# A transformer layer with retention, pooling and a convolutional MLP: score matmuls by row halves, other places of weight splits, an output stage in another order, a tail that works in PSUM

## The chip, the cores and the metric

The kernel runs on one core of one Trainium2 chip. The metric is the device time of one execution in microseconds, from the chip's own clock; of several executions the median is taken. A core has five engines that run side by side, each with its own instruction stream in a fixed order: PE (TensorE, matrix products, written into eight banks of PSUM), DVE (VectorE), ACT (ScalarE), POOL (GpSimd), and SP (SyncE), which here only issues transfers between HBM and SBUF. An instruction waits by semaphores for what it reads and for the buffers that it overwrites, and everything behind it on its engine waits with it.

## What is computed

One layer over 512 latent tokens (x, 512 x 1024) with 256 context tokens, all in float32. Cut to what matters:

```python
u = _layer_norm(x) * (1.0 + sc1) + sh1                 # sh, sc, g: SiLU(c) @ w_ada + b_ada, six rows
k, v, q, g, p_in, gate_a, gate_b = split(u @ w_in)     # context tokens: k and v alone
# retention: 8 heads, key width 64, value width 128, chunks of 128 tokens, two directions
scores = einsum('bnihd,bnjhd->bnhij', qc, kc) * decay_in
y = scores @ vc + (q * q_dec) @ s_prev                 # both directions, per-head norm, times silu(g)
ret = y @ w_branch_ret
pool = pool_mixer(p_in) @ w_branch_pool
mix = (sigmoid(gate_a) * ret + sigmoid(gate_b) * pool) @ w_out
x = _layer_norm(ALPHA * x + g1 * mix) * ln1_g + ln1_b
u2 = _layer_norm(x) * (1.0 + sc2) + sh2
h = depthwise_conv3x3(u2 @ w_up) + conv_b              # 5632 channels on an 8 x 64 grid
a, b = split(h)
x = _layer_norm(ALPHA * x + g2 * ((gelu(a) * b) @ w_down)) * ln2_g + ln2_b
```

## The kernel before

Each float32 product is made of three matmuls (`mm3`, lines 92 to 95): both operands are split into a rounded part (`hi`, written by ACT) and the rest (`lo`, a subtraction on DVE or POOL, line 83), and hi*hi, hi*lo and lo*hi are summed in PSUM. Weights come from HBM into rotating `raw` buffers (six) or `row` buffers (three), are split into `hi` and `lo` (two buffers each) and used once. In the steps of `run_steps` the split of the next weight is written ahead of the product of the present one.

The stages in order of time are: the modulation and norm of x, the first projections, k and v, then eight steps `ga_step` and eight `gb_step` (one 512-wide product each, 24 matmuls) that carry the retention of one head per step: `ret_a(h)` makes the head's scores, states and decayed queries, `ret_b(h)` and `ret_c(h)` a step later the output, its norm and its transposes. In `ret_a` one head's scores are four matmuls with 64 rows (line 632), since a head's q and k lie in one half of the 128 partitions: even heads in rows 0 to 63, odd heads in rows 64 to 127 of tile `t`. From `k_post` to the end of the `br` steps only SP is in the written order; a scheduler has placed the instructions of the other engines when the program was built.

Then eight `br_step` (24 matmuls each) and eight `bp_step` (12 matmuls each) merge the branches. Among them `prep_out` (line 755) loads and splits the eight row tiles of `w_out` for the output projection into four buffers `wo[0]` to `wo[3]`; the tables `BR_W` and `BP_W` name the step at which each one is prepared. `wo[2]` and `wo[3]` take the buffers S6 and S0, which hold the split input of the `br` steps until the last of these has ended. In the `bp` steps PE and SP are in the written order, the rest is scheduled.

The output stage is written out by hand for all engines: for each block `tb` of 128 tokens two products of 24 matmuls (`out_mm`), whose halves stay in PSUM (`zps`); residual and statistics on DVE; `out_x1a` (mean and `ln_scale`, whose two small instructions on POOL, lines 125 and 126, give the reciprocal deviation; a multiplication by ln1_g on DVE), `out_x1b` (the scale and ln1_b, statistics of the next norm, and again `ln_scale`), `out_norm` (the normalised block into `xr`), `out_tr` (eight transposes on PE, then modulation on ACT, and the `lo` part by POOL or DVE). In the shadow of this, `early_prep` splits the first six weights of the up-projection, and `first_half` multiplies them with the first two blocks (24 matmuls of 256 columns).

After the up-projection, the convolution and most of the down-projection (18 of 22 row tiles for all blocks) the tail goes block by block: `unit` makes the last four row tiles' products for a half of 512 columns (12 matmuls), `gated_add` multiplies by g2 into an SBUF buffer and adds it to `x1`; `quarters`, `norm_a` and `norm_b` are the statistics, the mean and ln2_g, and the scale, ln2_b and store. The last block's second half is made in two quarters of 256 columns.

```python
def prep_out(i, k):
    ...
    raw = load(row() if i >= 2 else raw4(), a["w_out"][2 * i + k])
    act.copy(w[:, 0, k, :], raw)
    sub(dve if k and i < 3 else pool, w[:, 1, k, :], raw, w[:, 0, k, :].bitcast(F32))
```

Of the kernel before, what the change touches and what calls it, by code (L numbers as in the profile page):

```python
# [45 lines left out]
def layer_kernel(ctx: ExitStack, tc: tile.TileContext, a: dict):  # L46
# [707 lines left out]
    def prep_out(i, k):  # L754
# [113 lines left out]
    def out_norm(tb):  # L868
        src = x1[:, tb, :]
# [250 lines left out]
    for f in range(2, N_FRONT):  # L1120
# [14 lines left out]
    def gated_add(z, ps, cs, eng, add):  # L1135
        t = t2((P, cs.stop - cs.start))
        if eng is act:
            act.copy(t, ps)
            pool.tensor_tensor(t, t, g2[:, cs], ALU.mult)
        else:  # L1140
            dve.tensor_tensor(t, ps, g2[:, cs], ALU.mult)
        add.tensor_tensor(z[:, cs], z[:, cs], t, ALU.add)
# [2 lines left out]
    gated_add(x1[:, end, :], banks[end][1], HALVES[1], act, pool)
    st = [t2((P, 4, 6)) for _ in range(NTB)]
    scale = {}

    def unit(tb, cs):
# [122 lines left out]
```

## Time and profile before

| | us |
|---|---|
| three runs | 844.09, 845.35, 846.95 |
| median | 845.35 |
| the profiled execution | 847.08 |
| its span, first to last instruction | 845.3 |
| PE busy | 811.7 |
| DVE busy | 545.3 |
| POOL busy | 405.8 |
| ACT busy | 363.3 |

The mean granted clock of TensorE over the span is 0.985 of full speed. The span leaves 1.8 us of the profiled execution outside. A timeline row gives the start in us from the span's beginning, the duration, engine, line and operation, output and inputs by the program's names without their numbers, the count of merged instructions, and in brackets how long the engine had idled before it and what ended that. PE's matmuls overlap in the pipeline, so their pace is read from the starts, not from the durations. Float32 matmuls that are not split (scores, states, transposes of other data) appear as two records each.

### The profile page before, as it was taken

The numbers are of one execution on the slowest core, as the hardware profiler recorded it, in microseconds if no ns is written. First come the engines' busy times: TensorE is split into PE (matmuls) and PEld (weight loads), VectorE is DVE, ScalarE is ACT, GpSimd is POOL, SyncE is SP. The second block draws the span as 40 slices with busy tenths as digits, with TensorE's granted clock in tenths as the row PEclk, the third lists the DMA queues.
The fourth block names the chain that finished last, engine by engine and source line by source line (L and its number), as shares of the span: only waits on it lengthen the run. The fifth ranks groups of instructions, "written<-read, shape, count | busy, mean of one in ns | idle before, by whom it ended". The sixth has DMA issues, their size and how long they took to land.

```text
span 845.3 us, 10601 instructions
## 1 busy us (share of the span) xinstructions
PE 811.7 (96%) x3865; PEld 676.7 (80%) x3865; DVE 545.3 (65%) x1033; ACT 363.3 (43%) x578; POOL 405.8 (48%) x303
## 2 busy tenths in 40 slices
PE   6989999999999999998999899999999999999993
PEld 4768877888888888887887898888888888888883
DVE  7948789783267773444566659877788877522148
ACT  4644527121544342323233557666666665233100
POOL 3745350030633230204333859988888888222145
PEclk9999999999999999999999999999999999999997
DMA  9940369864210006352404512232232223342002
GB/s 347 406 173 13 136 230 324 305 224 139 74 51 26 2 1 224 125 174 83 176 26 171 188 42 75 100 100 100 100 100 94 88 93 100 121 137 93 0 1 99
DMA packets 34068, 106.94 MB, mean 127 GB/s; under 512 B 4560, under 2 KB 5344, under 8 KB 34016
## 3 DMA queue, kind: packets, MB, share of 16 engines
q1 hardware_dynamic: 34016, 106.27, 35.9%
q8 instruction: 30, 0.49, 0.2%
q14 instruction: 22, 0.18, 0.1%
HBM read 104.14 MB, written 2.11 MB: 126 GB/s over the span
## 4 chain that ended last, share of the span: by engine, by line
PE 82%; DVE 7%; POOL 4%; ACT 3%; issue 2%; DMA 1%; SPq 0%; POOLq 0%; DVEq 0%
PE ps L95 24%; PE ps L94 24%; PE ps L93 24%; PE ps L356 3%; POOL S L83 2%; PE ps L632 1%; PE ps L668 1%; PE ps L669 1%; PE ps L638 1%; ACT t L896 1%; PE ps L635 1%; DVE raw L205 1%; DVE lo L83 1%; DMA S<-in_x 1%; PE ps L298 1%
## 5 line engine op out<-in xcount | busy, mean ns | idle before, releaser
L95 PE MATMUL ps<-S,lo 128*128 128x512 f32 (+1 forms) x560 | 217.4, 390 | 5.6 <-POOL lo L83 4.6
L93 PE MATMUL ps<-S,hi 128*128 128x512 f32 (+1 forms) x560 | 218.6, 390 | 1.0 <-ACT hi L88 1.0
L94 PE MATMUL ps<-S,hi 128*128 128x512 f32 (+1 forms) x560 | 217.4, 388 | 0.0
L83 POOL TENSOR_TENSOR lo<-raw,hi 128x1024 fp32r<-128x1024 f32 (+2 forms) x65 | 141.1, 2172 | 158.5 <-ACT hi L88 155.6
L990 DVE SCALAR_TENSOR_TENSOR t<-ps,convw,t 128x441 f32<-128x441 f32 (+1 forms) x258 | 163.9, 692 | 46.3 <-POOL t L988 46.1
L88 ACT CAST hi<-raw 128x1024 fp32r<-128x1024 f32 (+2 forms) x100 | 100.0, 1001 | 181.5 <-PE ps L95 67.7
L95 PEld LDWEIGHTS ps<-S,lo 128*128 128x128 f32 x560 | 106.0, 189 | 28.6 <-POOL lo L83 5.4
L93 PEld LDWEIGHTS ps<-S,hi 128*128 128x128 f32 x560 | 106.1, 189 | 22.6 <-ACT hi L88 1.5
L94 PEld LDWEIGHTS ps<-S,hi 128*128 128x128 f32 x560 | 106.0, 189 | 21.1
L988 POOL TENSOR_TENSOR t<-t,t 128x448 f32<-128x448 f32 x88 | 101.9, 1158 | 36.6 <-ACT t L1071 33.1
L94 PE MATMUL ps<-S,S 128*128 128x512 f32 (+1 forms) x308 | 112.4, 365 | 0.0
L95 PE MATMUL ps<-S,S 128*128 128x512 f32 (+1 forms) x308 | 112.3, 365 | 0.0
L93 PE MATMUL ps<-S,S 128*128 128x512 f32 (+1 forms) x308 | 111.7, 366 | 0.0
L83 DVE TENSOR_TENSOR lo<-raw,hi 128x1024 fp32r<-128x1024 f32 x37 | 50.0, 1351 | 70.0 <-ACT hi L88 69.9
L94 PE MATMUL ps<-lo,S 128*128 128x512 f32 x208 | 81.8, 393 | 0.0
L95 PE MATMUL ps<-hi,S 128*128 128x512 f32 x208 | 81.5, 393 | 0.0
L93 PE MATMUL ps<-hi,S 128*128 128x512 f32 x208 | 77.4, 392 | 1.7 <-ACT S L546 1.0
L83 POOL TENSOR_TENSOR S<-raw,S 128x1024 fp32r<-128x1024 f32 x21 | 50.5, 2405 | 43.5 <-ACT S L759 28.1
L1068 ACT ACTIVATE t<-ps,convb,convw 128x512 f32<-128x512 f32 x43 | 33.6, 781 | 76.5 <-PE ps L95 76.5
L95 PEld LDWEIGHTS ps<-S,S 128*128 128x128 f32 x308 | 58.3, 189 | 9.3
L94 PEld LDWEIGHTS ps<-S,S 128*128 128x128 f32 x308 | 58.4, 190 | 9.2
L93 PEld LDWEIGHTS ps<-S,S 128*128 128x128 f32 x308 | 58.4, 190 | 9.1
(212 smaller groups left out, 1085.0 us busy)
## 6 DMA issues: line engine op xcount, KB each, us to landing
raw<-in_w_up SPq DMA_DIRECT2D x44, 512.0 KB, 3.4
raw<-in_wada SPq DMA_DIRECT2D x32, 512.0 KB, 5.2
raw<-in_w_down SPq DMA_DIRECT2D x22, 512.0 KB, 3.3
S<-in_wada SPq DMA_DIRECT2D x16, 512.0 KB, 9.1
raw<-in_w_v SPq DMA_DIRECT2D x16, 256.0 KB, 4.4
raw<-in_w_ga SPq DMA_DIRECT2D x8, 512.0 KB, 4.5
raw<-in_w_gb SPq DMA_DIRECT2D x8, 512.0 KB, 3.3
raw<-in_w_br SPq DMA_DIRECT2D x8, 512.0 KB, 4.5
```

The costliest lines, as they stand in the source:

```text
L83: eng.tensor_tensor(out, x, y, ALU.subtract)
L88: act.copy(hi, raw)
L93: pe.matmul(out, lhsT=sh, rhs=mh, start=first, stop=False)
L94: pe.matmul(out, lhsT=sh, rhs=ml, start=False, stop=False)
L95: pe.matmul(out, lhsT=sl, rhs=mh, start=False, stop=last)
L205: dve.scalar_tensor_tensor(out_junk, raw, 1.0, silu_c, ALU.mult, ALU.mult, accum_out=mod[:, j:j + 1])
L298: pe.transpose(ps[:, j * P:(j + 1) * P], xs[:, tb, k * P:(k + 1) * P], ident)
L356: pe.matmul(g0[f], lhsT=w[:, f * P:(f + 1) * P], rhs=m[:, kt, :], start=kt == 0 and i == 0, stop=kt == NKT - 1 and i == 2)
L632: pe.matmul(sc[:, ns], lhsT=kT[rows, t, ns], rhs=qT[rows, t, ns], start=True, stop=True)
L988: pool.tensor_tensor(o, o, i, ALU.add)
L990: dve.scalar_tensor_tensor(o, i, w, o, ALU.mult, ALU.add)
L1068: act.activation(acc, src, AF.Identity, bias=convb[:, i:i + 1], scale=convw[:, i, 4:5])
```

## The change

Five things are changed.

1. **Scores.** When an even head comes, both heads of tile `t` get a bank, and their eight score matmuls are issued in turns, rows 0 to 63 and rows 64 to 127. The odd head finds its scores in `score`.
2. **Weight splits.** `w_out`'s row tiles are prepared at `br` steps 0, 1, 3, 4 and `bp` steps 0, 2, 4, 6, where it was 2, 2, 5, 5 and 0, 0, 3, 3. The `lo` part of the second half of `wo[2]` moves from DVE to POOL.
3. **Output stage.** `out_x1a` of blocks 1, 2 and 3 stands ahead of the transposes or the `early_prep` that it stood behind. Block 3's x1 stays in PSUM; `out_norm(3)` reads it there, stands behind `out_tr(2)`, and ACT copies it into `x1` afterwards.
4. **Regions.** The up-projection's seventh weight is prepared inside the region of the output stage.
5. **Tail.** Products by g2, the sum with `x1`, and statistics per half work in PSUM on DVE; `+EPS` moves from POOL to DVE. Block 0 and block 2 are finished on ACT (scale and mean) and POOL (ln2_g, ln2_b), block 1 on DVE (mean, ln2_g), ACT and POOL, block 3 on DVE. DVE, ACT and POOL are in the written order there. Eight stores of half blocks take the place of two of whole and four of half blocks.

```diff
-BR_W, BP_W = (2, 2, 5, 5), (0, 0, 3, 3)
+BR_W, BP_W = (0, 1, 3, 4), (0, 2, 4, 6)
-ORDT = (E_SP,)
+ORDT = (E_SP, E_DVE, E_ACT, E_POOL)
...
-        sc = bank()
-        for n in range(NTB):
-            ns = slice(n * P, (n + 1) * P)
-            pe.matmul(sc[:, ns], lhsT=kT[rows, t, ns], rhs=qT[rows, t, ns], start=True, stop=True)
+        if r == 0:
+            for i in range(2):
+                score[h + i] = bank()
+            for n in range(NTB):
+                ns = slice(n * P, (n + 1) * P)
+                for i in range(2):
+                    half_rows = slice(i * DK, (i + 1) * DK)
+                    pe.matmul(score[h + i][:, ns], lhsT=kT[half_rows, t, ns], rhs=qT[half_rows, t, ns],
+                              start=True, stop=True)
+        sc = score.pop(h)
...
-        sub(dve if k and i < 3 else pool, w[:, 1, k, :], raw, w[:, 0, k, :].bitcast(F32))
+        sub(dve if k and i < 2 else pool, w[:, 1, k, :], raw, w[:, 0, k, :].bitcast(F32))
...
-            z = x1[:, tb, cs]
+            z = ps if tb == NTB - 1 else x1[:, tb, cs]
...
         if tb == NTB - 1:
-            for cs in HALF:
-                dve.tensor_scalar(xr[tb][:, cs], src[:, cs], mu, rs, ALU.subtract, ALU.mult)
+            for hf in range(2):
+                dve.tensor_scalar(xr[tb][:, HALF[hf]], zps[tb, hf], mu, rs, ALU.subtract, ALU.mult)
+            for hf in range(2):
+                act.copy(x1[:, tb, HALF[hf]], zps[tb, hf])
             return
...
     out_mm(1, 1)
+    out_x1a(1)
     out_tr(0)
     out_x(2)
-    out_x1(1)
+    out_x1b(1)
...
     early_prep(2, pool)
+    out_x1a(3)
     early_prep(3, pool)
-    out_x1a(3)
+    out_x1b(3)
     early_prep(4, pool)
-    out_x1b(3)
-    out_norm(3)
     early_prep(5, pool)
     first_half(0)
     first_half(1)
     out_tr(2)
+    out_norm(3)
...
+    part = banks[NTB - 1][1]
+    dve.tensor_tensor(part, part, g2[:, HALVES[1]], ALU.mult)
+    dve.tensor_tensor(x1[:, NTB - 1, HALVES[1]], part, x1[:, NTB - 1, HALVES[1]], ALU.add)
...
+    def residual(tb, ps, cs):
+        dve.tensor_tensor(ps, ps, g2[:, cs], ALU.mult)
+        dve.tensor_tensor(ps, ps, x1[:, tb, cs], ALU.add)
+
+    def piece(tb, cs, n, of):
...
+        residual(tb, ps, cs)
...
+        dve.bn_stats(st[tb][:, n, :], ps)
+        parts[tb].append((ps, cs))
+
+    def block_scale(tb):
+        mv = small([P, 2])
+        dve.bn_aggr(mv, st[tb])
+        rs = small([P, 1])
+        dve.tensor_scalar(rs, mv[:, 1:2], EPS, None, ALU.add)
+        pool.tensor_tensor(rs, rs, neg_half, ALU.pow)
...
+    def centred(tb):
+        for ps, cs in parts[tb]:
+            dve.scalar_tensor_tensor(ps, ps, mean[tb], lng[:, cs], ALU.subtract, ALU.mult)
+
+    def finish_pool(tb):
+        nmr = small([P, 1])
+        dve.tensor_scalar(nmr, mean[tb], scale[tb], -1.0, ALU.mult, ALU.mult)
+        for ps, cs in parts[tb]:
+            act.activation(x1[:, tb, cs], ps, AF.Identity, bias=nmr, scale=scale[tb])
+        for ps, cs in parts[tb]:
             z = x1[:, tb, cs]
...
+            pool.tensor_tensor(z, z, lng[:, cs], ALU.mult)
+            pool.tensor_tensor(z, z, lnb[:, cs], ALU.add)
+            store(tb, cs)
+            yield
...
     for tb in range(end):
...
+        piece(tb, HALVES[0], 0, 2)
+        if tb == 1:
+            weave(finish_pool(0))
+        elif tb:
+            finish_act(tb - 1)
+        piece(tb, HALVES[1], 1, 2)
+        block_scale(tb)
+        if tb == 1:
+            centred(tb)
+    piece(end, HALVES[0], 0, 3)
+    late = finish_pool(end - 1)
+    next(late)
+    piece(end, QUARTERS[2], 1, 3)
+    piece(end, QUARTERS[3], 2, 3)
+    block_scale(end)
+    centred(end)
+    for i, (ps, cs) in enumerate(parts[end]):
+        dve.scalar_tensor_tensor(x1[:, end, cs], ps, scale[end], lnb[:, cs], ALU.mult, ALU.add)
+        if i != 1:
+            store(end, HALVES[min(i, 1)])
+        weave(late)
```

What the change does to the order on the engines is shown at three places. On PE, heads 2 and 3 of the retention, before (first fence) and now (second; line 636 is the new place of line 632, 641 and 644 of 635 and 638; `S0` is the tile with q and k, `S4` and `S6` hold v of the context and of the tokens):

```order
L95 MATMUL ps_316_2038<-S2_8_78,lo_300_1939 128x512
L632 MATMUL ps_319_2072<-S0_80_529 128x128 x4
L635 MATMUL ps_320_2077<-S4_169_1031,kdc_318_2067 128x128 x2
L638 MATMUL ps_321_2080<-S6_84_542,t2_317_2064 128x128 x4
...
L95 MATMUL ps_335_2144<-S2_8_78,lo_315_2035 128x512
L632 MATMUL ps_338_2178<-S0_80_529 128x128 x4
L635 MATMUL ps_339_2183<-S4_169_1031,kdc_337_2173 128x128 x2
```

```order
L95 MATMUL ps_316_2038<-S2_8_78,lo_301_1944 128x512
L636 MATMUL ps_319_2072<-S0_80_529 128x128
L636 MATMUL ps_320_2073<-S0_80_529 128x128
L636 MATMUL ps_319_2072<-S0_80_529 128x128
L636 MATMUL ps_320_2073<-S0_80_529 128x128
...
L641 MATMUL ps_321_2082<-S4_169_1031,kdc_318_2067 128x128 x2
...
L95 MATMUL ps_336_2149<-S2_8_78,lo_315_2035 128x512
L641 MATMUL ps_339_2183<-S4_169_1031,kdc_338_2178 128x128 x2
```

The four matmuls of head 3 (`ps_320` now) have moved up between those of head 2; at head 3's own place none are left.

On POOL, around the end of the `br` steps, before and now (`lo` of 128x512 is the split of the next `bp` weight; `S0` and `S6` are `wo[3]` and `wo[2]`):

```order
L83 TENSOR_TENSOR lo_494_3240<-raw_492_3237,hi_493_3239 128x512
L83 TENSOR_TENSOR S0_513_3340<-row_514_3341,S0_513_3340 128x1024
L83 TENSOR_TENSOR S6_498_3262<-row_499_3263,S6_498_3262 128x1024
L83 TENSOR_TENSOR lo_503_3274<-raw_501_3271,hi_502_3273 128x512
L83 TENSOR_TENSOR lo_507_3297<-raw_505_3294,hi_506_3296 128x512
L83 TENSOR_TENSOR S0_513_3340<-row_515_3345,S0_513_3340 128x1024
```

```order
L83 TENSOR_TENSOR lo_494_3240<-raw_492_3237,hi_493_3239 128x512
L83 TENSOR_TENSOR S0_517_3363<-row_518_3364,S0_517_3363 128x1024
L83 TENSOR_TENSOR S6_498_3262<-row_499_3263,S6_498_3262 128x1024
L83 TENSOR_TENSOR S6_498_3262<-row_508_3313,S6_498_3262 128x1024
L83 TENSOR_TENSOR lo_502_3270<-raw_500_3267,hi_501_3269 128x512
L83 TENSOR_TENSOR lo_506_3293<-raw_504_3290,hi_505_3292 128x512
L83 TENSOR_TENSOR S0_517_3363<-row_527_3414,S0_517_3363 128x1024
```

Between the `lo` of `bp` step 1 (`lo_494`) and that of `bp` step 2 stood two splits of 1024 columns, and now stand three; the third was DVE's.

On POOL, in the output stage from the statistics of block 3 on, before and now (`S7` and `S3` are the early up-projection weights, `S8` the `lo` part of the transposed blocks):

```order
L83 TENSOR_TENSOR S7_586_3812<-raw_585_3810,S7_586_3812 128x1024
L83 TENSOR_TENSOR S7_586_3812<-raw_587_3815,S7_586_3812 128x1024
L125 TENSOR_SCALAR sm_589_3821<-sm_588_3819 128x1
L126 TENSOR_TENSOR sm_589_3821<-sm_589_3821,neg_half_66 128x1
L83 TENSOR_TENSOR S3_591_3828<-raw_590_3826,S3_591_3828 128x1024
L125 TENSOR_SCALAR sm_594_3838<-sm_593_3836 128x1
L126 TENSOR_TENSOR sm_594_3838<-sm_594_3838,neg_half_66 128x1
```

```order
L83 TENSOR_TENSOR S7_586_3812<-raw_585_3810,S7_586_3812 128x1024
L125 TENSOR_SCALAR sm_588_3817<-sm_587_3815 128x1
L126 TENSOR_TENSOR sm_588_3817<-sm_588_3817,neg_half_66 128x1
L83 TENSOR_TENSOR S7_586_3812<-raw_589_3822,S7_586_3812 128x1024
L125 TENSOR_SCALAR sm_592_3833<-sm_591_3831 128x1
L126 TENSOR_TENSOR sm_592_3833<-sm_592_3833,neg_half_66 128x1
L83 TENSOR_TENSOR S3_594_3838<-raw_593_3836,S3_594_3838 128x1024
```

Each pair of small instructions (lines 125 and 126) of block 3 has moved ahead of one split of 1024 columns.

## Rows read from the trace of the kernel before

**Rows 1.** Windows of the core: length, busy time (instructions) of each engine, clock, DMA.

```profile
200.00:300.00 100.00, 100.00 (x576) 85.28 (x575) 55.38 (x150) 38.96 (x86) 34.07 (x26) 1.00 0.13 43
...
750.00:800.00 50.00, 50.00 (x223) 41.38 (x222) 9.81 (x8) 15.47 (x15) 9.60 (x4) 1.00 0.22 70
...
832.00:846.00 14.00, 0.00 (x0) 0.00 (x0) 9.38 (x15) 1.34 (x2) 7.25 (x7) 0.58 0.29 110
```

**Rows 2.** Timeline of PE around the scores of one head.

```profile
233.24 0.39 PE L95 MATMUL ps<-S,lo 128*128 128x512 f32 x1
233.55 1.16 PE L632 MATMUL ps<-S 64*128 64x128 f32 x8
234.64 0.71 PE L635 MATMUL ps<-S,kdc 128*128 128x128 f32 x4
235.19 1.06 PE L638 MATMUL ps<-S,t 128*128 128x128 f32 x8
236.08 0.60 PE L613 MATMUL ps<-ident,S 128*128 128x128 f32 x4
```

**Rows 3.** Timeline of PE at the third `bp` step.

```profile
397.45 0.39 PE L94 MATMUL ps<-S,hi 128*128 128x512 f32 x1
400.71 0.80 PE L95 MATMUL ps<-S,lo 128*128 128x512 f32 x1 [2.87 <-POOL lo L83]
...
404.22 0.39 PE L94 MATMUL ps<-S,hi 128*128 128x512 f32 x1
```

**Rows 4.** Timeline of POOL at the same place.

```profile
392.46 1.30 POOL L83 TENSOR_TENSOR lo<-raw,hi 128x512 fp32r<-128x512 f32 x1 [4.15 <-ACT hi L88]
393.71 5.72 POOL L83 TENSOR_TENSOR S<-row,S 128x1024 fp32r<-128x1024 f32 x2
399.39 2.50 POOL L83 TENSOR_TENSOR lo<-raw,hi 128x512 fp32r<-128x512 f32 x2
401.86 2.37 POOL L83 TENSOR_TENSOR S<-row,S 128x1024 fp32r<-128x1024 f32 x1
```

**Rows 5.** Timeline of DVE at the same place.

```profile
395.32 1.89 DVE L83 TENSOR_TENSOR S<-row,S 128x1024 fp32r<-128x1024 f32 x1
```

**Rows 6.** Timeline of PE in the output stage, its two waits.

```profile
452.92 1.09 PE L888 MATMUL ps<-ident,xr 128*128 128x128 f32 x8 [0.90 <-ACT xr L877]
...
476.97 0.28 PE L95 MATMUL ps<-S,S 128*128 128x256 f32 x1
479.32 1.09 PE L888 MATMUL ps<-ident,xr 128*128 128x128 f32 x4 [2.07 <-issue]
...
481.45 0.56 PE L93 MATMUL ps<-S,S 128*128 128x256 f32 x1
```

**Rows 7.** Timeline of POOL in the output stage, two of its small instructions.

```profile
446.38 0.22 POOL L125 TENSOR_SCALAR sm<-sm 128x1 f32<-128x1 f32 x1
...
471.64 0.22 POOL L125 TENSOR_SCALAR sm<-sm 128x1 f32<-128x1 f32 x1
```

**Rows 8.** Timeline of DVE in the output stage.

```profile
423.93 0.70 DVE L844 TENSOR_TENSOR ps<-ps,row 128x512 f32<-128x512 f32 x1 [2.20 <-PE ps L95]
...
447.28 0.75 DVE L860 SCALAR_TENSOR_TENSOR S<-ps,sm,row 128x512 f32<-128x512 f32 x1 [3.16 <-POOL sm L126]
...
472.55 0.75 DVE L860 SCALAR_TENSOR_TENSOR S<-ps,sm,row 128x512 f32<-128x512 f32 x1 [2.22 <-POOL sm L126]
...
476.65 3.98 DVE L873 TENSOR_SCALAR xr<-S,sm,sm 128x512 f32<-128x512 f32 x2 [1.00 <-POOL sm L126]
```

**Rows 9.** Timeline of PE, its last matmul.

```profile
831.49 0.28 PE L95 MATMUL ps<-S,S 128*128 128x256 f32 x1
```

**Rows 10.** Timeline of DVE in the tail.

```profile
836.01 0.40 DVE L1141 TENSOR_TENSOR t<-ps,row 128x256 f32<-128x256 f32 x1
...
840.87 1.41 DVE L1174 SCALAR_TENSOR_TENSOR S<-S,sm,row 128x512 f32<-128x512 f32 x2 [0.77 <-POOL sm L126]
```

**Rows 11.** Timeline of SP's queue, the last two stores.

```profile
841.65 0.99 SPq L1175 DMA_DIRECT2D out_x<-S  x2
```

More of the change, by code (lines that the diff above doesn't have):

```diff
@@ L606, in layer_kernel @@
     yg = slot(1, [P, H, SEQ])
-    ktok, pend = {}, {}
+    ktok, pend, score = {}, {}, {}
     qds = [None]
@@ L876, in out_norm @@
         dve.tensor_scalar(nmr, mu, rs, -1.0, ALU.mult, ALU.mult)
-        act.activation(xr[tb], src, AF.Identity, bias=nmr, scale=rs)
+        act.activation(xr[tb], x1[:, tb, :], AF.Identity, bias=nmr, scale=rs)
     def out_tr(tb):
@@ L951, in layer_kernel @@
     out_mm(2, 1)
+    out_x1a(2)
     out_tr(1)
     out_x(3)
-    out_x1(2)
+    out_x1b(2)
     out_norm(2)
@@ L972, in layer_kernel @@
     first_half(5)
-    inner.__exit__(None, None, None)
-    ordered(*ORDS)
     acts = [slot(s, [P, 8, SEQ], F32R) for s in (2, 7, 6, 5, 3, 0)]
@@ L1058, in layer_kernel @@
     up_prep(n_early)
+    inner.__exit__(None, None, None)
+    ordered(*ORDS)
     for i in range(2 * NFF):
@@ L1131, in layer_kernel @@
             tc.keep_in_program_order(act.activation(x1[:, i, :], x1[:, i, :], AF.Copy, scale=ALPHA))
+    part = banks[NTB - 1][1]
+    dve.tensor_tensor(part, part, g2[:, HALVES[1]], ALU.mult)
+    dve.tensor_tensor(x1[:, NTB - 1, HALVES[1]], part, x1[:, NTB - 1, HALVES[1]], ALU.add)
     ordered(*ORDT)
     QUARTERS = tuple(slice(i, i + CTX) for i in range(0, D, CTX))
[L1135 to L1142, printed above, removed]
-    end = NTB - 1
[L1145 to L1149, printed above, removed]
-        hf = cs.start // SEQ
-        apart = tb == end and hf == 1
-        ps = bank()[:, 0:CTX] if apart else banks[tb][hf]
+    end = NTB - 1
+    st, mean, scale, parts = {}, {}, {}, {}
+    def residual(tb, ps, cs):
+        dve.tensor_tensor(ps, ps, g2[:, cs], ALU.mult)
+        dve.tensor_tensor(ps, ps, x1[:, tb, cs], ALU.add)
+    def piece(tb, cs, n, of):
+        apart = tb == end and cs.start >= SEQ
+        ps = bank()[:, 0:CTX] if apart else banks[tb][cs.start // SEQ]
         for f in range(N_FRONT, NFF):
@@ L1155, in unit @@
                     apart and f == N_FRONT, f == NFF - 1)
-        gated_add(x1[:, tb, :], ps, cs, dve, dve if apart else pool)
-    def quarters(tb, cs):
-        for q in range(cs.start // CTX, cs.stop // CTX):
-            dve.bn_stats(st[tb][:, q, :], x1[:, tb, QUARTERS[q]])
-    def norm_a(tb):
-        mu, scale[tb] = ln_scale(st[tb])
-        z = x1[:, tb, :]
-        dve.scalar_tensor_tensor(z, z, mu, lng, ALU.subtract, ALU.mult)
-    def norm_b(tb, eng, pieces=(slice(0, D),)):
-        for cs in pieces:
-            z = x1[:, tb, cs]
-            if eng is act:
-                act.activation(z, z, AF.Copy, scale=scale[tb])
-                pool.tensor_tensor(z, z, lnb[:, cs], ALU.add)
-            else:
-                dve.scalar_tensor_tensor(z, z, scale[tb], lnb[:, cs], ALU.mult, ALU.add)
-            dma.dma_start(a["out"][tb * P:(tb + 1) * P, cs], z)
@@ L1195, in layer_kernel @@
-    norm_a(end)
-    norm_b(end, dve, HALVES)
+        residual(tb, ps, cs)
+        if n == 0:
+            st[tb] = t2((P, of, 6))
+            parts[tb] = []
+        dve.bn_stats(st[tb][:, n, :], ps)
[6 more added lines that the diff above has]
+        pool.tensor_tensor(rs, rs, neg_half, ALU.pow)
+        mean[tb], scale[tb] = mv[:, 0:1], rs
@@ new lines, in store @@
+    def store(tb, cs):
+        dma.dma_start(a["out"][tb * P:(tb + 1) * P, cs], x1[:, tb, cs])
+    def centred(tb):
[7 more added lines that the diff above has]
+        for ps, cs in parts[tb]:
+            z = x1[:, tb, cs]
+            pool.tensor_tensor(z, z, lng[:, cs], ALU.mult)
+            pool.tensor_tensor(z, z, lnb[:, cs], ALU.add)
+            store(tb, cs)
+            yield
@@ new lines, in finish_act @@
+    def finish_act(tb):
+        for ps, cs in parts[tb]:
+            z = x1[:, tb, cs]
+            act.activation(z, ps, AF.Copy, scale=scale[tb])
+            pool.tensor_tensor(z, z, lnb[:, cs], ALU.add)
+            store(tb, cs)
+    for tb in range(end):
+        piece(tb, HALVES[0], 0, 2)
[7 more added lines that the diff above has]
+            centred(tb)
```

18 lines of the change are left out of this document (removed).

## The prediction, written before the result was known

> **What bounds the kernel now.** I read the windows first, then PE's timeline for every idle stretch, then the engine that ended each. PE is busy without a break over most of the span: 100 of 100 us in the retention, 50 of 50 in the down-projection, where 223 records in 50 us (a few are missing) give a pace of 0.227 us for a matmul of 512 columns [rows 1]. So an edit counts only if it takes PE time away, ends a wait of PE, or shortens what follows PE's last matmul. In the stretches that the change touches PE waits at three places: 2.87 us at the third `bp` step, for POOL [rows 3]; 0.90 and 2.07 us ahead of transposes in the output stage [rows 6]; and from 832 on it has nothing left to do, while DVE works 9.4 of 14 us [rows 1]. The last matmul starts at 831.49, so it ends at 831.77 [rows 9]; DVE gets to its result only at 836.01 and finishes at 842.28 [rows 10]. DVE, not PE, bounds the tail.
>
> **Scores: 4.2 us gained.** A head's four score matmuls are eight records from 233.55 to 234.64, 1.09 us or 0.136 each; the full-height matmuls of line 638 are paced at 0.89 / 8 = 0.111 [rows 2]. Around the block PE loses more: the first score comes 0.31 after the last matmul instead of 0.227, and the four records of line 635 behind it take 0.55 where 0.111 each would be 0.44, so 0.08 + 0.11 = 0.19 a block [rows 2]. Eight heads cost 8.7 us of a PE that never rests there [rows 1]. Of the eight blocks four remain: 4 x 0.19 = 0.8 gained in every case in which the halves are one mode. No row shows two matmuls in different halves at once, so the rest is bounded. If only the weight loads are hidden and the records still come one after the other, the pace falls to 0.111: 64 x 0.025 = 1.6. If the second head is free: 4 x 1.09 = 4.4. Between: two records of one head stay in sequence, the other head lags by one record, so a pair takes 9 steps of 0.136 = 1.22 instead of 2.18, or 3.8 for four pairs. That makes 4.6; the first pair is cut in two by the gate product's matmuls in the built order, which gives back an entry and a step, some 0.35. I take 4.2, with ends of 0 and 5.1, nearer the upper one because rows, banks and data of the two halves are apart.
>
> The row shows no overlap between a score and its neighbour [rows 2]. The Trainium skill (TensorE: Matmul & The Clock Gate, Part 3, Packing small matmuls) says that matmuls in different row groups run at the same time, a pack lasting as long as one plus about 4 ns for each further tile; by it a pair would take about 1.1 us and the gain would be some 4.2 + 0.8 = 5.0, by the pace alone 2.4.
>
> **Weight splits: 1.5 us lost.** The table spreads the splits, but the built order puts three of 1024 columns between the `lo` of `bp` step 1 and that of step 2, where two stood: `wo[3]` still comes early, and the second half of `wo[2]` moves from DVE, where it took 1.89 [rows 5], to POOL. The buffers are free only when the `br` steps have ended, so none can start sooner. POOL's two took 5.72, that is 2.86 each, with DVE's split beside them; one without took 2.37 [rows 4]. With DVE's gone I take 2.40: POOL starts at 393.71, ends three at 400.9, and the 512-wide `lo` (1.25 [rows 4]) at 402.15, where it was 399.39 + 1.25 = 400.64. PE's matmul at 400.71 moves by 1.5. At 2.86 each it would be 2.9. The clock comes on top: after that wait eight matmuls from 400.71 to 404.22 took 3.51 us, not 8 x 0.227 = 1.81, so PE ran at half speed, the lower level of 1.2 GHz, and lost 1.7 [rows 3]. The same loss is in the forecast; it could go, or double. Ends: 0.2 gained, 4.6 lost. Behind the third split also the `lo` of step 3 and the last split of `wo[3]` come 1.5 later; PE is later by as much, so nothing new waits. The splits in the `br` steps find POOL idle and the `raw` buffers free in time, since the transfers keep their distance of several steps: zero. If that cover were gone, one wait of 1 to 3 us would come up there.
>
> **Output stage: 4.9 us gained.** `out_x1a`'s small instruction on POOL for block 1 ran at 446.38, behind the two subtractions of `out_tr(0)`, though its statistics were ready at about 442.7 (this and the other times of this part that stand without a row are sums over the same queues); DVE waited 3.16 for it [rows 7, 8]. Now it stands ahead of them: `out_x1b(1)` starts some 3 us sooner, `xr` of block 1 is there before 450, and the 0.90 us wait is gone. Nobody pays: the subtractions on POOL come 0.9 later and their reader is the up-projection. Block 3: the small instruction ran at 471.64 behind two weight splits, and DVE waited until 472.55 [rows 7, 8]. Now one split stands ahead, and ACT can feed it once block 2's norm is through, about 461; `out_x1b(3)` follows DVE's own work at about 467.8, 4.7 sooner. Then the normalised block: 3.98 for two halves out of SBUF, while POOL was splitting [rows 8]; out of PSUM I take 0.70 each, as for another operation on a bank [rows 8], so 2.6 less (at the old price it would be 0). `xr` of block 3 is ready at about 473.3 instead of 480.6. PE wants it at 477.1, less the 0.9 from above: 2.9 us of slack. So the whole of the second wait goes: from 476.97 to 481.45 PE did one matmul (0.12) and eight transposes (8 x 0.111 = 0.89 at full pace), 3.5 of the 4.48 were lost [rows 6], and about 0.5 more since the first matmul afterwards took 0.56, twice the 0.28 of the last one before [rows 6]. 0.9 + 3.5 + 0.5 = 4.9. ACT's two new copies (an estimate: 0.7 each) free the banks that `first_half(4)` and `(5)` take; they end at about 475.5, PE arrives at 476.9. Late next is the `lo` part of blocks 2 and 3 on POOL, behind all weight splits: about 480.5, wanted at 482.6. If that slack of 2 is gone, the gain shrinks by what is missing. Ends: 3.0 and 5.3.
>
> **Tail: 2.7 us gained.** PE keeps its order and ends at 831.77; counting back by 2.72 (12 x 0.227) a half and 1.44 a quarter, the halves of blocks 1 to 3 end at 820.7, 823.5, 826.2 and 828.9. On a bank each DVE operation costs 0.70, with its gap 0.73 [rows 8], so product, sum and statistics of a half are 2.2; a quarter, by 0.40 [rows 10] and gaps, 1.3; the aggregate and `+EPS` 0.55. From 820.8 DVE works without a pause: block 1's second half 2.2, its scale 0.55, its mean and ln2_g 1.5; 825.0; block 2 4.95; 829.95; block 3's first half and a small one 2.45; 832.4; two quarters 2.6 and the scale 0.55; 835.55. Then mean and ln2_g of three pieces 1.6 and scale and ln2_b 1.6: 838.75, where it was 842.28. POOL has two additions or products of 1.3 for each finished half (1.30 [rows 4], with gap 1.37): block 0 until 826.8, block 1's two until 830.9, block 2's first half until 835.8, the last small instruction until 836.4, then block 2's second half until 839.15. Its store stands ahead of the last one on SP: 839.2, then a second issue; the two issues of before took 0.99 with their wait between [rows 11], so the last one is out at about 839.95 instead of 842.65. The end follows by the same 2.65: 2.7 gained. With DVE alone as the bound it would be 3.5; with POOL's operations stretched by 0.4 each, 1.5.
>
> **Sum.** -4.2 + 1.5 - 4.9 - 2.7 = -10.3. The profiled execution took 847.08 (span 845.3 and 1.8 around it): 836.8. It lies 1.73 above the median of the runs, so against the median of 845.35: **835.0**. The regions and the seventh weight's place count nothing: all engines are in the written order on both sides of the boundary, and that weight is wanted 16 us later.
>
> **Rivals.** (1) The halves don't overlap: pace only, or no gain at all: 4.2 becomes 2.4 or 0, so 836.8 to 839.2. For it: no row shows an overlap. Against: 0.136 against 0.111 says that something is exposed which the other half could cover. (2) The splits do what the table says, and the wait at the third `bp` step goes with its slow matmuls: 3.03 + 1.7 gained instead of 1.5 lost, 828.8. Against: the built order. (3) The slack behind the output stage is used up: the up-projection's second halves wait on POOL, the gain is 2 to 3: 837.5. For it: POOL gets its `lo` parts last. (4) Slower: an odd head's scores now hold a bank for a head longer. If PE then waits for a bank once a pair, and pays as at the `bp` step (2.87 idle and 1.7 of slow clock [rows 3]), four pairs cost 18 us: 853. It decides from 3.2 us a pair, which eats up 10.3 and 2.5 more. Against: DVE, which empties the banks, is busy for 55 of 100 us there [rows 1], and in the built order each such bank is next written by work that stands many matmuls behind the reader. The Trainium skill (TensorEngine Tiling (Array Packing), Gotcha 1: PSUM Pressure) warns that row tiling needs more banks; no row here shows PE waiting for one.
>
> **How the numbers follow.** A measurement of this kernel tells 0.3%, or 2.5 us, from no change. Forecast 0.72 (831 to 839), (1) 0.13, (2) 0.03, (3) 0.08, (4) 0.04. The ends of the terms add to -14.1 at best (831.2) and nothing at worst, which needs all four to miss. Leaving out (2) and (4) and a little at both sides gives 830.5 to 840.0. Faster by over 0.3% (below 842.8) 0.93, within 0.3% 0.03, slower 0.04.
>
> **What would show it.** Scores: sixteen records of a pair within 1.1 to 1.4 us; 1.8 or 2.2 would be rival 1. `bp`: PE's wait ends at 402.2 in the old time, 4.4 us long instead of 2.87. Output stage: no wait of PE ahead of any transposes. Tail: DVE ends about 7 us behind PE's last matmul, not 10.5, and the last store is of block 3, behind one of block 2. Wrong would be the whole if PE showed idle stretches between 220 and 330, where it has none now.

## The result and the profile after

The changed kernel took 833.54 us (median of four runs, 832.83 to 834.19), the kernel before 846.1 (four runs, 844.09 to 846.95): a ratio of 0.9855, interval 0.9833 to 0.9876. By the ratio that is 12.3 us less (the medians differ by 12.6), where the prediction had 10.3, and 833.5 where it had 835.0. The profiled execution took 833.84 us; its span is 832.0 and the mean granted clock 0.989, where 845.3 and 0.985 stood before.

Four places of the trace of the changed kernel answer the rows read before. Its lines are numbered anew: the scores are line 636 (632 before), the states 641 and 644, `out_x1b` 866, block 3's norm 878, transposes of the output stage 895.

**Scores** [rows 2]. PE's timeline, first an even head, which carries both heads' scores, then an odd one from earlier in the trace:

```profile
240.83 1.16 PE L636 MATMUL ps<-S 64*128 64x128 f32 x16
241.92 0.71 PE L641 MATMUL ps<-S,kdc 128*128 128x128 f32 x4
242.47 1.06 PE L644 MATMUL ps<-S,t 128*128 128x128 f32 x8
...
231.69 0.61 PE L641 MATMUL ps<-S,kdc 128*128 128x128 f32 x4
```

From 240.83 to 241.92 sixteen records take 1.09 us, what eight took before. Taken one by one, the second head's records start 7 ns behind the first's; the row shows no other cost of the second head.

**Weight splits** [rows 3, 4]. PE and POOL at the third `bp` step:

```profile
390.57 0.39 PE L94 MATMUL ps<-S,hi 128*128 128x512 f32 x1
395.18 0.79 PE L95 MATMUL ps<-S,lo 128*128 128x512 f32 x1 [4.22 <-POOL lo L83]
...
401.27 0.39 PE L94 MATMUL ps<-S,hi 128*128 128x512 f32 x1
```

```profile
386.84 7.06 POOL L83 TENSOR_TENSOR S<-row,S 128x1024 fp32r<-128x1024 f32 x3
393.87 2.49 POOL L83 TENSOR_TENSOR lo<-raw,hi 128x512 fp32r<-128x512 f32 x2
```

Three splits of 2.35 us each stand ahead of the `lo` that PE waits for; the wait has grown from 2.87 to 4.22. Behind it fourteen matmuls, and no longer eight, run at half speed: from 395.18 to 401.27 they stand 0.43 us apart, and the granted clock of this stretch is 0.51, the lower level of 1.2 GHz.

**Output stage** [rows 6 to 8]. The windows of the core (length, busy time and instructions of PE, PEld, DVE, ACT, POOL, clock, DMA share, GB/s), then POOL's small instruction of block 1 ahead of the two subtractions, then POOL's of block 3, DVE's `out_x1b` of blocks 1 and 3 and block 3's norm, and the transposes that read it:

```profile
440.00:484.00 44.00, 44.00 (x299) 40.74 (x299) 24.68 (x42) 21.67 (x39) 25.44 (x23) 1.00 0.49 180
```

```profile
438.44 0.22 POOL L125 TENSOR_SCALAR sm<-sm 128x1 f32<-128x1 f32 x1 [3.01 <-DVE sm L123]
...
439.28 2.68 POOL L83 TENSOR_TENSOR S<-t,S 128x512 fp32r<-128x512 f32 x2
...
462.00 0.22 POOL L125 TENSOR_SCALAR sm<-sm 128x1 f32<-128x1 f32 x1 [1.49 <-DVE sm L123]
```

```profile
439.72 0.74 DVE L866 SCALAR_TENSOR_TENSOR S<-ps,sm,row 128x512 f32<-128x512 f32 x1
...
463.27 0.75 DVE L866 SCALAR_TENSOR_TENSOR ps<-ps,sm,row 128x512 f32<-128x512 f32 x1
...
467.38 1.53 DVE L878 TENSOR_SCALAR xr<-ps,sm,sm 128x512 f32<-128x512 f32 x2 [1.00 <-POOL sm L126]
...
471.64 1.04 PE L895 MATMUL ps<-ident,xr 128*128 128x128 f32 x8
```

PE is busy for all 44 us; both waits are gone, and the clock stays at full speed. DVE no longer waits for POOL ahead of line 866 (3.16 and 2.22 us before), and block 3 is normalised at 468.91, 2.7 us before PE wants it.

**Tail** [rows 9 to 11]. PE's last matmul; DVE, POOL and SP behind it:

```profile
821.95 0.28 PE L95 MATMUL ps<-S,S 128*128 128x256 f32 x1
```

```profile
824.82 1.53 DVE L1180 SCALAR_TENSOR_TENSOR ps<-ps,sm,row 128x512 f32<-128x512 f32 x3
826.26 1.52 DVE L1219 SCALAR_TENSOR_TENSOR S<-ps,sm,row 128x512 f32<-128x512 f32 x3
```

```profile
827.22 1.26 POOL L1190 TENSOR_TENSOR S<-S,row 128x512 f32<-128x512 f32 x1
```

```profile
828.51 0.81 SPq L1176 DMA_DIRECT2D out_x<-S  x2
```

DVE ends at 827.78, 5.55 us behind PE's last matmul, where it ended 10.5 behind. POOL's last addition for block 2 ends at 828.48 and is now later than DVE. Of the last two stores the first carries its result and goes out 0.03 us behind it; the second, of block 3, stands behind that one on SP, although DVE was done at 827.78. The span ends 9.81 us behind the last matmul, before 13.53.

**Stage by stage.** Whole executions scatter by some us, so I cut each profiled span at five points that no edit touches: the first key transposition on PE (line 613), the last `br` product and the first product by g1 on DVE (767 and 844 of before), the first convolution on ACT (1068), and the end of PE's last matmul. All in us; the up-projection to the last matmul is 340.8 in every kernel and left out.

| kernel | to first k | retention, `br` | `bp`, first product | output stage | behind PE |
|---|---|---|---|---|---|
| before | 219.53 | 172.46 | 31.94 | 67.02 | 13.53 |
| after | 217.51 | 167.60 | 34.52 | 61.78 | 9.81 |
| e1_scores | 217.51 | 167.61 | 31.99 | 68.78 | 13.54 |
| e2_splits | 217.24 | 172.46 | 34.56 | 67.60 | 13.53 |
| e3_output | 219.12 | 172.45 | 31.98 | 61.80 | 13.53 |
| e4_tail | 220.48 | 172.46 | 32.02 | 67.56 | 9.81 |
| f1_pool_order | 220.07 | 167.60 | 27.84 | 61.78 | 9.81 |
| f2_dve_split | 217.84 | 167.60 | 31.97 | 61.78 | 9.82 |
| f3_in_a_row | 219.60 | 169.72 | 33.88 | 61.79 | 9.83 |
| g1_norm_sbuf | 218.63 | 167.58 | 34.40 | 62.34 | 9.81 |
| g2_first_part_late | 218.19 | 167.60 | 34.31 | 61.78 | 9.83 |
| g3_blocks_1_2_late | 219.12 | 167.58 | 33.28 | 62.88 | 9.82 |
| b1_tables | 219.44 | 167.60 | 27.84 | 61.77 | 9.82 |
| b2_tail | 217.97 | 167.58 | 27.75 | 61.78 | 9.77 |

The stretch up to the first key transposition, which the change leaves alone, lies between 217.2 and 220.5: this is most of the scatter of whole executions. The other stages repeat within 0.1 us, except where PE has waited. So between the two profiled executions the change itself gave -4.86 + 2.58 - 5.24 - 3.72 = -11.2; the other 2.0 of the 13.3 in the spans were luck at the start.

### The profile page after: what moved, and what is told of

It is laid out like the page before. It is cut to its first block, busy times and chain, and to the rows that moved or that the text cites. A ratio compares the mean times of both kernels' runs of the same rounds, so it can differ in the third digit from the quotient of the medians.

```text
span 832.0 us, 10613 instructions
## 1 busy us (share of the span) xinstructions
PE 804.0 (97%) x3865; PEld 670.9 (81%) x3865; DVE 537.6 (65%) x1040; ACT 365.7 (44%) x583; POOL 402.1 (48%) x299
## 4 chain that ended last, share of the span: by engine, by line
PE 50%; DVE 1%; POOL 1%; POOLq 0%; issue 0%; ACT 0%
PE ps L95 17%; PE ps L94 17%; PE ps L93 16%; PE ps L895 0%; DVE ps L1151 0%; DVE ps L1150 0%; POOL S L1189 0%; DVE t L1164 0%; DVE ps L1180 0%; POOLq L1294 0%; POOL S L1190 0%; ACT S L1186 0%; POOL sm L1172 0%; DVE sm L1169 0%; DVE sm L1171 0%
## 5 line engine op out<-in xcount | busy, mean ns | idle before, releaser
L83 DVE TENSOR_TENSOR lo<-raw,hi 128x1024 fp32r<-128x1024 f32 x37 | 47.6, 1286 | 67.2 <-ACT hi L88 67.1
```

The lines of the kernel that those rows point to most:

```text
L83: eng.tensor_tensor(out, x, y, ALU.subtract)
```

## The experiments

**Each part alone.** Four kernels, each the kernel before with one part of the change. The edits are the parts 1, 2, 3 with 4, and 5 of the diff above:

```
e1_scores: + for n in range(NTB): for i in range(2): pe.matmul(score[h + i][:, ns], ...)
e2_splits: + BR_W, BP_W = (0, 1, 3, 4), (0, 2, 4, 6)    + sub(dve if k and i < 2 else pool, ...)
e3_output: + out_x1a(1) ahead of out_tr(0), ...         + z = ps if tb == NTB - 1 else x1[:, tb, cs]
e4_tail:   + piece, block_scale, centred, finish_pool, finish_act; ORDT with DVE, ACT, POOL
```

> The kernel before with the scores alone changed (two heads' matmuls in turns, rows 0 to 63 and 64 to 127); all else stays. Theory (the second head is free): four pairs save 4 x 1.09 us, and four of the eight blocks' entries and exits 4 x 0.19: 5.1 us less than before, less some 0.2 for the first pair, which is cut in two. Records of a whole pair: sixteen in about 1.1 us. Rival (only the weight loads are hidden, the records still come one after the other): 2.4 us less. Rival (banks held longer make PE wait): slower.

> The kernel before with the places of the w_out splits alone changed (tables, and the lo part of wo[2]'s second half on POOL). Theory: three splits of 1024 columns ahead of the third bp step's lo make PE wait about 4.2 us, where it waited 2.9, and the half-speed stretch behind the wait lasts 14 matmuls, where it lasted 8 (+1.2): 2.6 us slower than before. Rival (only the wait grows, as the prediction had it): 1.5 slower. Rival (the wait goes): 4.7 faster.

> The kernel before with the output stage alone changed (first parts of the norms ahead, block 3 in PSUM) and the seventh weight inside that region. Theory: both waits ahead of transposes go with their slow matmuls: 5.2 us less than before, no idle PE between 423 and 491. Rival (the slack behind is used up, the up-projection's second halves wait on POOL): 2 to 3 less.

> The kernel before with the tail alone changed. Theory: from the end of PE's last matmul to the end of the span 13.5 us become 9.8, and nothing ahead of it moves: 3.7 us less than before. Rival (as the prediction summed it, DVE 7 us behind PE): 2.7 less. If the four single edits add to about -11.4, no edit leans on another; if the whole change gains more than their sum, the rest is interplay or lies ahead of all of them.

Measured against 845.53 for the kernel before: e1_scores 841.39, ratio 0.994 (0.992 to 0.9961), or -5.1; e2_splits 848.59, 1.0028 (1.0017 to 1.004), or +2.4; e3_output 840.81, 0.9929 (0.991 to 0.9948), or -6.0; e4_tail 842.01, 0.9958 (0.9943 to 0.9972), or -3.6. They add to -12.3, which is the whole change: within these intervals, 1.0 to 1.7 us to either side, no part leans on another, and the table shows each in its own stage and nowhere else. Part 4 was run only together with part 3, and the steps of part 5 only together, so what each of them is worth by itself isn't shown. The sum that I had put down, -11.4, was short in the output stage. The reason stands in PE's timeline of e1_scores, behind the second wait of the old output stage:

```profile
472.46 0.63 PE L894 MATMUL ps<-ident,xr 128*128 128x128 f32 x4 [2.04 <-issue]
473.83 1.12 PE L894 MATMUL ps<-ident,xr 128*128 128x128 f32 x4 [0.73 <-DVE xr L879]
474.59 0.56 PE L93 MATMUL ps<-S,S 128*128 128x256 f32 x1
474.95 0.41 PE L94 MATMUL ps<-S,S 128*128 128x256 f32 x1
...
479.65 0.40 PE L95 MATMUL ps<-S,S 128*128 128x256 f32 x1
479.86 0.30 PE L93 MATMUL ps<-S,S 128*128 128x256 f32 x1
```

From 474.95 to 479.86 the matmuls of 256 columns follow each other at 0.21 us, where from 480.0 on they need 0.12; the granted clock of the stretch is 0.50, the lower level. In the profiled execution of before only the first four behind that wait were slow, in e2_splits and e4_tail eleven, here twenty-four. The old stage cost 67.0 to 68.8 us with the same instructions and nearly the same waits, 67.74 on average of the four; the new one 61.77 to 61.80 in every execution without a wait. So the gain is 6.0, not the 5.2 of the two profiled executions.

**What makes the wait at the `bp` step.** Two edits of the changed kernel:

```
f1_pool_order: - ORDB = (E_PE, E_SP)                + ORDB = (E_PE, E_SP, E_POOL)
f2_dve_split:  - sub(dve if k and i < 2 else pool,  + sub(dve if k and i < 3 else pool,
```

> The changed kernel, with POOL too in the written order from the bp steps on: its splits then stand as the tables say, one of 1024 columns between two lo parts, not three ahead of the third lo. Theory (the three splits are the wait, and the wait is the slow stretch behind it): the wait of 4.2 us and its 14 matmuls at half speed (2.9) go, 7.1 us less than the changed kernel, some 826.5; from br_7's product on DVE to the first one of the output projection 27.4 us instead of 34.5. Rival (POOL can't deliver four splits and eight lo parts in the time of the bp steps, the wait only moves): 2 to 5 less. Rival (another thing holds PE there, the buffers or ACT): no gain.

> The changed kernel with only the engine of the one split put back (the lo part of wo[2]'s second half on DVE again), tables as changed. Theory (the engine makes the loss, the tables do nothing): two splits ahead again, wait 2.9 and 8 slow matmuls, 2.6 us less than the changed kernel, the stretch 31.9 us. Rival (the tables make it): no difference.

f1_pool_order took 827.91, 0.9787 of the kernel before (0.9768 to 0.9807); f2_dve_split 831.62, 0.9827 (0.9807 to 0.9847). POOL and PE of f1_pool_order at the third `bp` step:

```profile
390.09 2.41 POOL L83 TENSOR_TENSOR S<-row,S 128x1024 fp32r<-128x1024 f32 x1 [0.65 <-POOL lo L83]
392.45 2.55 POOL L83 TENSOR_TENSOR lo<-raw,hi 128x512 fp32r<-128x512 f32 x2
...
393.81 0.50 PE L95 MATMUL ps<-S,lo 128*128 128x512 f32 x1 [0.28 <-POOL lo L83]
...
394.93 2.44 POOL L83 TENSOR_TENSOR S<-row,S 128x1024 fp32r<-128x1024 f32 x1
```

One split of 1024 columns now stands ahead of the `lo`, not three; the wait is 0.28 us, no matmul behind it runs at half speed, and the stretch is 27.84 instead of 34.52. The theory holds (27.4 expected). This kernel beats the kernel before and the changed one: its interval lies below both. In f2_dve_split POOL, DVE and PE stand as in the kernel before:

```profile
387.17 5.73 POOL L83 TENSOR_TENSOR S<-row,S 128x1024 fp32r<-128x1024 f32 x2
...
388.77 1.89 DVE L83 TENSOR_TENSOR S<-row,S 128x1024 fp32r<-128x1024 f32 x1
...
394.17 0.50 PE L95 MATMUL ps<-S,lo 128*128 128x512 f32 x1 [2.88 <-POOL lo L83]
```

The wait is 2.88 and the stretch 31.97, as with the old tables. So the engine of one split made the whole loss, and the tables alone neither helped nor hurt, because the scheduler put the splits in front whatever step the table named.

**Two heads in a row.** The edit swaps the two loops around the score matmuls of the changed kernel:

```
- for n in range(NTB):         + for i in range(2):
-     for i in range(2):       +     for n in range(NTB):
```

> The changed kernel with the two heads' scores in one block still, but four matmuls of one head and then four of the other, not in turns. Theory (only neighbours in different halves run at once): a pair takes about 2.1 us instead of 1.09, 4.1 us more than the changed kernel. Rival (the halves run side by side however they are issued): no difference.

837.43, 0.989 (0.9871 to 0.9909); the stage is 169.72, 2.12 longer than in turns. PE's timeline of one pair:

```profile
243.40 1.71 PE L636 MATMUL ps<-S 64*128 64x128 f32 x16
245.04 0.71 PE L641 MATMUL ps<-S,kdc 128*128 128x128 f32 x4
```

A pair takes 1.64 us: neither the 2.1 of the theory nor the 1.09 of its rival. Half of the second head runs beside the first even in this order, and only in turns all of it does. Taken one by one, the sixteen starts fall into two rows of eight at the same pace: one from 243.40 to 244.28, the other from 243.95 to 244.83. The record at 244.28 raises PE's semaphore, as the first head's last matmul does in the program, so the first row is the first head. The second head's first matmul thus starts 0.55 us behind the first head's, before the first head's last one has started. Why it starts there and not earlier, this run doesn't show.

**What ends the second wait of the output stage.** The change makes block 3 earlier in three ways; each is undone alone in the changed kernel:

```
g1_norm_sbuf:       - z = ps if tb == NTB - 1 else x1[:, tb, cs]    + z = x1[:, tb, cs]
g2_first_part_late: - out_x1a(3); early_prep(3); out_x1b(3); early_prep(4)
                    + early_prep(3); out_x1a(3); early_prep(4); out_x1b(3)
g3_blocks_1_2_late: - out_x1a(1); out_tr(0); out_x(2)               + out_tr(0); out_x(2); out_x1a(1)
                    (and so for block 2)
```

> The changed kernel with block 3's x1 written to SBUF again and its norm read from there (no copies by ACT); the first parts stay ahead. Theory (the earlier start is what ends the wait): the norm's two halves take some 4 us instead of 1.5 and end at about 471.4 in the time of the changed kernel, where PE wants them at 471.6: no wait, no difference, or a wait of a few tenths. Rival (reading PSUM is what ends it): a wait of 1 us or more with slow matmuls behind, 1.5 to 3 us more.

> The changed kernel with block 3's two small POOL instructions back behind one weight split more each, its norm still in PSUM. Theory (the first parts carry the gain, the norm in PSUM gives 2.5 of the 4.7 + 2.5 us by which the block is earlier): the normalised block comes at about 472.9 where PE wants it at 471.6, a wait of about 1.3 us and a few slow matmuls: 1.5 to 3.5 us more than the changed kernel. Rival (the norm in PSUM alone does it): no difference, no wait.

> The changed kernel with the first parts of blocks 1 and 2 back behind the transposes of the block before; block 3 as changed. Theory (the gain of block 3 too comes from block 2, whose norm on ACT holds back the weight splits that stand in front of block 3's small instruction on POOL): the wait of 0.9 us with its exit comes back, everything of block 3 is some 3.5 to 4 us later, ready at 472.5 to 473 where PE then wants it at 472.6: 1.2 to 1.8 us more than the changed kernel. Rival (block 3's own move carries its part): 1.2 more and no second wait. Rival (nothing but the norm in PSUM counts): no difference.

The times (835.51, 0.9864 with 0.985 to 0.9877; 834.32, 0.9854 with 0.9834 to 0.9873; 835.56, 0.987 with 0.9855 to 0.9885) can't be told from that of the changed kernel; the stage can: 62.34, 61.78 and 62.88 against 61.78. POOL, DVE and PE of g1_norm_sbuf; POOL of g2_first_part_late; PE and DVE of g3_blocks_1_2_late:

```profile
468.29 4.93 POOL L83 TENSOR_TENSOR S<-raw,S 128x1024 fp32r<-128x1024 f32 x2
468.36 5.15 DVE L878 TENSOR_SCALAR xr<-S,sm,sm 128x512 f32<-128x512 f32 x2 [1.00 <-POOL sm L126]
...
473.56 0.66 PE L893 MATMUL ps<-ident,xr 128*128 128x128 f32 x4 [0.33 <-DVE xr L878]
```

```profile
463.44 0.22 POOL L125 TENSOR_SCALAR sm<-sm 128x1 f32<-128x1 f32 x1
```

```profile
448.97 1.09 PE L895 MATMUL ps<-ident,xr 128*128 128x128 f32 x8 [0.93 <-ACT xr L884]
...
470.41 1.53 DVE L878 TENSOR_SCALAR xr<-ps,sm,sm 128x512 f32<-128x512 f32 x2 [1.00 <-POOL sm L126]
```

No edit alone brings the wait of 2.07 us back. Out of SBUF the norm takes 5.15 us instead of 1.53, and PE waits 0.33. With block 3's small instruction behind two splits again, it runs only 1 us later in its stage (43.3 us behind the stage's first product, 42.4 in the changed kernel, 47.7 before): no wait at all, against my theory of 1.3. With blocks 1 and 2 late the wait of 0.93 comes back (1.1 us in all), and block 3 is still in time: the rival, not the theory. With its own move alone, in g3, block 3's small instruction comes 45.4 us behind the stage's first product: of the 5.3 us by which the change makes it earlier, blocks 1 and 2 alone give 4.4 and its own move alone 2.3. So any two of the three end the second wait, but for 0.33 us, and each is covered by the slack that the other two leave; the first wait, ahead of block 1's transposes, comes back only in g3_blocks_1_2_late, which has the first parts of blocks 1 and 2 late.

**Two more steps on the best kernel.** On top of f1_pool_order:

```
b1_tables: - BP_W = (0, 2, 4, 6)     + BP_W = (1, 3, 5, 6)
b2_tail:   b1_tables, and in the tail
           - dve.tensor_scalar(nmr, mean[tb], scale[tb], ...)     + pool.tensor_scalar(nmr, ...)
           block 2's scale on POOL ahead of the second addition of block 1
```

> The changed kernel with POOL in the written order from the bp steps on, and the last four splits prepared at bp steps 1, 3, 5, 6, so that the lo of the third step stands ahead of any of them. Theory: the 0.28 us of wait that the written order alone left go too, the stretch from br_7's product to the output projection's first one is 27.4 us; 0.45 less than with the written order alone, 7.1 less than the changed kernel. Rival (the wait moves to a later step's lo): as with the written order alone, or 1 to 2 more.

> As b1_tables, and in the tail the small instructions of block 2 earlier on POOL: its scale ahead of the second addition of block 1, and the product of mean and scale on POOL instead of DVE. Theory (POOL's last addition, at 828.5, is what ends last, and it is late because ACT waits for that product behind DVE's work on block 3): POOL ends 1 us sooner, DVE's end at 827.8 is the bound, 0.5 to 0.7 us less from the last matmul to the end (9.8 becomes 9.1 to 9.3). Rival (the last store, not POOL, sets the end): no change of that stretch.

829.35, 0.9791 (0.9777 to 0.9805), and 827.61, 0.9779 (0.9765 to 0.9792): neither can be told from f1_pool_order. POOL and PE of b1_tables, then POOL of b2_tail:

```profile
390.95 1.29 POOL L83 TENSOR_TENSOR lo<-raw,hi 128x512 fp32r<-128x512 f32 x1 [2.13 <-ACT hi L88]
392.20 2.41 POOL L83 TENSOR_TENSOR S<-row,S 128x1024 fp32r<-128x1024 f32 x1
394.56 2.54 POOL L83 TENSOR_TENSOR lo<-raw,hi 128x512 fp32r<-128x512 f32 x2
...
395.91 0.50 PE L95 MATMUL ps<-S,lo 128*128 128x512 f32 x1 [0.29 <-POOL lo L83]
```

```profile
815.25 0.28 POOL L1184 TENSOR_SCALAR sm<-sm,sm 128x1 f32<-128x1 f32 x1
...
820.84 1.26 POOL L1190 TENSOR_TENSOR S<-S,row 128x512 f32<-128x512 f32 x1
```

In b1_tables the third step's `lo` is in time, and the same 0.29 us of wait stands at the fourth step, whose `lo` now follows a split: the rival. In b2_tail the product ends at 815.53, 0.4 us before PE's last matmul ends (815.90); in b1_tables, on DVE, it ended 0.3 before. Standing on POOL behind block 1's second addition it was no earlier, and POOL's end stays 6.2 us behind PE's. The edit missed its aim, but SP's queue shows how theory and rival hang together: as in the changed kernel, the store of POOL's last half goes out 0.03 us behind POOL's end (822.13 behind 822.10), block 3's follows it at 822.56 though DVE is done at 821.44, and the span ends 2.7 us after that store has been issued, as it does before the change. So POOL's end holds up the last store, and the end follows the store; what POOL ending sooner would give was not measured.

## Why the prediction was right, and where it was off

The sum of terms was -10.3. Corrected for the scatter behind waits (`bp` stretch 34.16 as the mean of the six kernels with three splits ahead, 31.98 of the five with two; output stage as above) the parts are -4.86 + 2.2 - 6.0 - 3.7 = -12.4, and the time ratio says -12.3 (-10.5 to -14.1).

**Scores, -4.2 forecast, -4.86 measured.** The mechanism was right and the size between the two bounds was not: I took a lag of one record, 0.136 us, and gave some back for the cut pair; the records show a lag of 7 ns. The Trainium skill (TensorE: Matmul & The Clock Gate, Part 3, Packing small matmuls) has a pack of row tiles last as long as one matmul plus about 4 ns for each further tile; by it a pair takes about 1.1 us, and the 1.09 agrees. The same part of the Trainium skill has matmuls start and end in program order, strictly first in, first out. In f3_in_a_row a matmul of the second head starts at 243.95 us, ahead of the first head's last one (244.17), which stands before it in the program; so this run doesn't agree. Rival 1 (no overlap) and rival 4 (PE waits for banks) are refuted, the one by the 1.09 us, the other since PE is busy for 100 of 100 us from 200 to 300, as in [rows 1]:

```profile
200.00:300.00 100.00, 100.00 (x606) 86.31 (x605) 59.51 (x166) 38.46 (x86) 35.32 (x28) 1.00 0.11 38
```

**Weight splits, +1.5 forecast, +2.2 measured (2.6 in the profiled execution).** Three splits on POOL at 2.35 (2.40 forecast) and a wait of 4.22 (4.4 forecast): right, and f2_dve_split shows that the moved split is the cause. The step that failed is "the same loss is in the forecast": the half-speed stretch was kept at eight matmuls. Behind the wait of 2.9 it was seven or eight in each of five kernels; behind 4.2 it was fourteen, fourteen, thirteen, thirteen, ten and seven (starts 0.35 us apart or more). The granted clock shows what differs, the moment at which it falls and that at which it rises. In the changed kernel it is at the lower level from 394.4 on, 0.8 us before the wait ends; in f3_in_a_row it falls 2.2 us before the end, so that part of the low stretch passes while PE waits, and some ten matmuls are left; in g3_blocks_1_2_late it falls with the end and is back after seven; in e4_tail, whose wait is 2.87 us, it falls 1.4 us after the end. What sets these moments isn't shown. Rival 2, that the table does what it says, was refuted for the changed kernel, and f1_pool_order shows what it would have been worth: 34.16 - 27.84 = 6.3 us. I had priced it against the old kernel, 3.03 + 1.7 gained; 31.98 - 27.84 = 4.1 is what it gives there.

**Output stage, -4.9 forecast, -6.0 measured.** Both waits went, block 3 was in time with the slack forecast (2.9; measured 2.7), and rival 3, a wait on POOL for the `lo` parts, didn't come: PE has no idle time there. The mis-sized term is the slow matmuls behind the second wait, put at 0.5 from the one execution that showed the least of them. The way was also not quite as told: I put the 4.7 us on block 3's own move and 2.6 on the norm; in g2_first_part_late the small instruction is 4.4 us earlier than before without that move, so most of it comes through blocks 1 and 2. In the kernel before (first fence) the casts of these weights stand on ACT behind block 2's norm (line 877), and POOL's splits wait for the casts; in the changed kernel (second) the casts, and with them the split ahead of the small instruction, come earlier, 38.5 us behind the stage's first product and not 42.9:

```profile
464.54 1.24 ACT L877 ACTIVATE xr<-S,sm,sm 128x1024 f32<-128x1024 f32 x1 [6.71 <-DVE sm L876]
465.69 3.88 ACT L925 CAST S<-raw 128x1024 fp32r<-128x1024 f32 x4
...
466.80 4.76 POOL L83 TENSOR_TENSOR S<-raw,S 128x1024 fp32r<-128x1024 f32 x2 [2.54 <-ACT S L925]
```

```profile
456.99 3.87 ACT L932 CAST S<-raw 128x1024 fp32r<-128x1024 f32 x4
...
458.10 2.42 POOL L83 TENSOR_TENSOR S<-raw,S 128x1024 fp32r<-128x1024 f32 x1 [2.54 <-ACT S L932]
```

And the norm out of SBUF cost 5.15 in g1_norm_sbuf, not 3.98: it stretches with what POOL does beside it. Taken one by one, DVE's two halves took 2.62 and 2.61 us there, and each ended 0.28 to 0.29 us behind one of POOL's two splits of 1024 columns (2.40 and 2.57), which had started just ahead of it; in the kernel before they took 2.57 and 1.49, and ended as closely behind a POOL instruction of 2.35 and one of 1.45. The Trainium skill (SBUF — State Buffer, Who interferes with whom) says that DVE in a two-port mode and GpSimd share one pair of ports that either holds for a whole instruction; these times agree with that. Reading PSUM, the norm takes 1.53 for both halves with a split of 2.41 on POOL beside it.

**Tail, -2.7 forecast, -3.72 measured.** I had each DVE operation on a bank start 0.73 behind the one before. That holds where it needs the result of the one before; where it works on another bank, it starts after 0.61. Statistics of one half, product of the next, sum of the next:

```profile
816.53 0.70 DVE L1164 BATCH_NORM_STATS2 t<-ps 128x6 f32<-128x512 f32 x1
817.14 0.68 DVE L1150 TENSOR_TENSOR ps<-ps,row 128x512 f32<-128x512 f32 x1
817.86 0.70 DVE L1151 TENSOR_TENSOR ps<-ps,S 128x512 f32<-128x512 f32 x1
```

Block 2 took 4.57 us (815.07 to 819.64) instead of 4.95, its neighbours likewise, and the chain ended 5.55 behind PE, not 7. POOL, forecast to end 7.4 behind PE's last matmul (839.15 less 831.77), ended 6.25 behind. As forecast POOL ends last, and the last store stands behind the store of its result; so DVE's gain of 4.96 became 3.72.

**The total** came out within 1.5 us of the forecast partly by luck: of the errors in the four terms, -0.7, +0.7, -1.1 and -1.0 us, the first two cancel, and of the -2.1 that remain 0.75 is covered because the median of before rose to 846.1 with a fourth run.

## What to carry to other kernels

Matmuls that use half of the rows should be issued in turns with the other half, not behind one another (1.09 against 1.64 us a pair here). A table that says when a piece of work is written says nothing about when it runs, unless the engine that does it is in the written order: look up where it stands in the built queue, and put a split that nobody waits for behind one that somebody does. A wait of PE should be priced with the slow matmuls behind it, from several executions, since one profile may show the cheapest case.

## What was not expected of the hardware

- The half-speed stretch behind a wait differs between executions with the same instructions: seven to fourteen matmuls of 512 columns behind 4.2 us of wait, four to twenty-four of 256 columns behind some 2.1 us and a second short wait. Without a wait the output stage takes 61.77 to 61.80 us in all eight kernels that have none.
- Two runs of four half-height matmuls, one behind the other, took 1.64 us, where one alone takes 1.09: the second starts 0.55 us behind the first, before the first has issued its last matmul.
- A normalisation of 128 x 512 out of SBUF took 1.49 to 2.62 us and ended 0.3 us behind the POOL instruction beside it in all four cases; out of PSUM it took 0.77.
